# Delta-rule keys transposed with the values, key norms from squares with accumulators

## The chip, the cores and the metric

The kernel runs on one NeuronCore of a Trainium2 chip. The metric is the device time of one execution in microseconds (us). The engines are named as in the profile: PE is the matrix engine (its weight loads are listed apart as PEld), DVE the vector engine, ACT the scalar engine, POOL the GpSimd engine, SP the engine whose queue issues the transfers from memory. SBUF is the on-chip memory that they all read, PSUM the banks that PE writes.

## The reference, cut to what matters

The reference is a decoder trunk of two layers over 256 tokens of 1024 channels. Each layer has a mixer (a delta-rule branch of 8 heads and a sliding-window attention branch of 16 query heads, merged by gates) and a gated feed-forward part. The change touches the delta-rule branch only:

```python
dn_qkv = jax.nn.silu(causal_dwconv(dn_qkv, dn_conv[l]))
dq, dk, dv = [t.reshape(B, T, DN_HEADS, DN_HEAD_DIM) for t in jnp.split(dn_qkv, 3, axis=-1)]
dq, dk = l2_norm(dq), l2_norm(dk)      # x * rsqrt(sum(x*x) + EPS) over the 128 channels of a head
...
# in the chunked delta rule, S is a 128x128 state of a head:
k_dec = kc * jnp.exp(g_last[..., None] - gc)[..., None]
v_new = u_i - jnp.einsum('bhcd,bhde->bhce', w_i, S)
S = S * jnp.exp(gl)[..., None, None] + jnp.einsum('bhcd,bhce->bhde', kd, v_new)
```

The keys are needed in two layouts: channels on the partitions (as the projection leaves them, for the products of keys with keys and queries), and tokens on the partitions (for the update of the state). The norm of a key is one number per token.

## The kernel before, in words

**Projections.** Everything that is projected is computed as tiles of 128 output channels by 256 tokens. A projection tile is 24 matmuls (lines L282, L283, L284, eight times each): activations and weights are split into a high and a low part, and three products are summed into one PSUM tile `acc`. A tile's weights come by one transfer of 512 KB on the queue of SP (L200, `raw`); ACT rounds them to the high part (L210, `wH`), and DVE subtracts to get the low part (L212, `wL`). These casts run up to three tiles ahead of the products. I number the projection tiles from 0 in the order of the program, and write "tile 12, product 0" for the place just before the first matmul of tile 12. The delta rule of the first layer works beside tiles 0 to about 50; the second layer's tiles begin at 142, and its delta rule ends near tile 190.

**The work between the projections.** A convolution tile (`conv_tile`) follows each of the 24 projection tiles of queries, keys and values: two ACT copies out of PSUM (L669, L670), three DVE steps (L672), one ACT silu (L674). Values end in `vv`, queries and keys in `kq`. When the three tiles of a head exist, a job `post` is started for it; when all four heads of a half are posted, a job runs `system`, `inverse` and `solve` for the half. In between, DVE reduces the conditioning weights of the next sub-layers (L328, `raw<-raw,cact`, 128x1024, on weights from the queue of SP too), and ACT and DVE prepare the attention (`attention_prep`, L962 to L967, then L975).

**What sets the order.** Jobs are generators. After each triple of projection matmuls the program calls `tick`, which resumes the job that is due; a job yields a cost and a wait, in assumed microseconds, that decide after how many triples it is resumed. So the yields at the end of `post` and of `system` place all that follows. Priorities (`HPC`, `HPV`, `HPN`, and the engines `AB`, `VB` that raise them) decide where an instruction stands among the instructions of its own engine. Each engine then runs its list strictly in that order. Helpers that raise a priority record their instructions under one line, L278.

**post, before (L688 to L708).** For a head: ACT squares the transposed-layout keys into `k2` (128x256, shown as `k<-kq`); PE transposes the two halves of the values into a PSUM tile (L703, `ps_vt`), and multiplies the squares with a column of ones, so that the sum over channels arrives on the partitions (L705, shown as `ps_n`; two products in full precision, which the trace records as four); ACT copies the values out (`vt`), and DVE adds EPS to the two sums (`n<-ps_n`, 128x2).

**system, before (L710 to L745).** For a half: DVE makes the inverse roots and the scales from `n2`; PE multiplies keys with keys and queries for each head (L728, `ps_kk`), DVE scales these (`lq`); ACT scales the values (`vt<-vt,nk`, eight of 128x128); PE transposes the first 128 tokens of the keys of four heads (L742, `ps_kt`), and ACT scales them out of PSUM into `kw`. `kw` is read in `solve` (L863).

**PSUM.** Three pools matter: `acc` with three buffers for the projections, `ps` with three for the delta rule's products, and `pat` with two, for `ps_vt` and `ps_n2` of `post`, for the transposed queries and keys of the attention (L962, L966) and for the attention's scores (`ps_cur`, L975). A buffer is free again when its last reader is done.

## Time and profile before

| What | Value |
|---|---|
| Time of three runs, median | 1029.28 us |
| Lowest and highest | 1028.52 and 1032.02 us |
| The profiled execution, span from first to last instruction | 1029.4 us |
| Its mean granted TensorE clock | 0.995 |
| PE busy | 999.7 us |
| DVE busy | 843.6 us |
| ACT busy | 631.2 us |

The profiled execution took as long as the median run, to 0.1 us, so its span is used for the time of the kernel throughout, with nothing around it.

In a timeline, a row gives the start of an instruction, its duration, the engine, the line, the operation, the tiles that it writes and reads, and shapes; equal neighbours are joined and counted (x4). In brackets stands how long the engine was idle before, and what ended that. Durations overlap the next instruction's, so a price is the distance from one start to the next: of two projection matmuls that is 0.11 to 0.12 us, though each lasts 0.28 us.

### The profile page before, as it was taken

To read this page: it belongs to the slowest core of one execution; us is meant where nothing else is said; L and a number is where in the kernel's file an instruction comes from. 1 tells how busy PE (TensorE), PEld (TensorE's weight loads), DVE (VectorE), ACT (ScalarE), POOL (GpSimd) and SP (SyncE) were. 2 spreads that over 40 slices of the span, in tenths; PEclk is the share of its full clock that TensorE was granted. 3 is DMA by queue.
4 is the path that set the end of the run, shared out by engine and by line. 5 is a ranking of instruction groups with operands and counts; after the bars stand their busy time and mean duration, and the time that the engine had idled before them with its cause. 6 is when DMAs were issued, how large, how long until landed. Compare 5 with 4: busy or idle time off the path is not lost.

```text
span 1029.4 us, 23195 instructions
## 1 busy us (share of the span) xinstructions
PE 999.7 (97%) x9208; PEld 946.0 (92%) x9208; DVE 843.6 (82%) x1873; ACT 631.2 (61%) x1281; POOL 4.0 (0%) x8
## 2 busy tenths in 40 slices
PE   4999999999999999999999999999999999999998
PEld 2599998998899999999999999899879999999998
DVE  6799997799788898998996999986857889777653
ACT  5598675766555665564465977577554558555532
POOL 0000000000000000000000000000000000000000
PEclk9999998999999999999999999999999999999999
DMA  9875486537555478888976556762313655566661
GB/s 361 324 247 175 173 268 204 183 124 266 170 183 191 155 226 282 291 282 298 358 262 210 168 168 193 239 242 83 110 57 107 202 185 179 191 191 194 185 211 40
DMA packets 60444, 210.47 MB, mean 204 GB/s; under 512 B 6960, under 2 KB 8496, under 8 KB 60336
## 3 DMA queue, kind: packets, MB, share of 16 engines
q1 hardware_dynamic: 59904, 208.89, 61.3%
q8 instruction: 72, 1.18, 0.5%
q14 instruction: 36, 0.29, 0.1%
q10 hardware_dynamic: 432, 0.10, 0.0%
HBM read 207.92 MB, written 1.05 MB: 203 GB/s over the span
## 4 chain that ended last, share of the span: by engine, by line
PE 77%; DVE 13%; ACT 5%; DMA 2%; issue 2%; SPq 0%; DVEq 0%; ACTq 0%
PE acc L282 20%; PE acc L283 19%; PE acc L284 19%; DVE wL L212 4%; PE pa L567 4%; DMA raw<-wada 2%; ACT wH L210 2%; DVE raw L328 2%; PE ps_o L1031 1%; PE ps_kk L728 1%; DVE kq L672 1%; PE ps_cur L975 1%; PE pa L585 1%; PE pa L583 1%; PE pa L584 1%
## 5 line engine op out<-in xcount | busy, mean ns | idle before, releaser
L210 ACT CAST wH<-raw 128x1024 fp32r<-128x1024 f32 (+2 forms) x292 | 301.0, 1035 | 207.8 <-PE acc L283 130.0
L212 DVE TENSOR_TENSOR wL<-raw,wH 128x1024 fp32r<-128x1024 f32 (+2 forms) x292 | 349.3, 1200 | 76.2 <-ACT wH L210 73.3
L282 PE MATMUL acc<-hH,wH 128*128 128x256 f32 x1376 | 394.3, 287 | 0.0
L283 PE MATMUL acc<-hL,wH 128*128 128x256 f32 x1376 | 385.8, 280 | 0.0
L284 PE MATMUL acc<-hH,wL 128*128 128x256 f32 x1376 | 385.1, 280 | 0.3 <-DVE wL L212 0.2
L282 PEld LDWEIGHTS acc<-hH,wH 128*128 128x128 f32 x1376 | 259.9, 189 | 7.4 <-issue 4.3
L284 PEld LDWEIGHTS acc<-hH,wL 128*128 128x128 f32 x1376 | 260.1, 189 | 1.1 <-DVE wL L212 0.7
L283 PEld LDWEIGHTS acc<-hL,wH 128*128 128x128 f32 x1376 | 260.1, 189 | 0.7 <-issue 0.2
L328 DVE SCALAR_TENSOR_TENSOR raw<-raw,cact 128x1024 f32<-128x1024 f32 x80 | 97.1, 1219 | 9.2 <-DMA raw<-wada 9.1
L284 PE MATMUL acc<-g_b,wL 128*128 128x256 f32 x224 | 61.8, 276 | 0.0
L282 PE MATMUL acc<-g_b,wH 128*128 128x256 f32 x224 | 61.8, 276 | 0.0
L283 PE MATMUL acc<-g_b,wH 128*128 128x256 f32 x224 | 61.8, 276 | 0.0
L672 DVE SCALAR_TENSOR_TENSOR kq<-cr,pt,kq 128x255 f32<-128x255 f32 (+2 forms) x96 | 45.4, 479 | 1.5 <-ACT kq L670 1.5
L282 PEld LDWEIGHTS acc<-g_b,wH 128*128 128x128 f32 x224 | 42.1, 188 | 0.0
L283 PEld LDWEIGHTS acc<-g_b,wH 128*128 128x128 f32 x224 | 42.1, 188 | 0.0
L284 PEld LDWEIGHTS acc<-g_b,wL 128*128 128x128 f32 x224 | 42.1, 188 | 0.0
L567 PE MATMUL pa<-raw,h 128*128 128x432 f32 x96 | 37.5, 555 | 2.6 <-ACT h L473 2.6
L1192 DVE SCALAR_TENSOR_TENSOR g<-acc,pt,g 128x255 f32<-128x255 f32 x80 | 38.2, 478 | 0.6
L567 PEld LDWEIGHTS pa<-raw,h 128*128 128x128 f32 x96 | 19.2, 202 | 20.6 <-issue 17.2
L282 PE MATMUL acc<-sH,wH 128*128 128x256 f32 x128 | 36.7, 289 | 0.0
L284 PE MATMUL acc<-sH,wL 128*128 128x256 f32 x128 | 36.6, 287 | 0.0
L283 PE MATMUL acc<-sL,wH 128*128 128x256 f32 x128 | 36.5, 285 | 0.0
(329 smaller groups left out, 1964.0 us busy)
## 6 DMA issues: line engine op xcount, KB each, us to landing
raw<-wbig SPq DMA_DIRECT2D x232, 512.0 KB, 4.0
raw<-wada SPq DMA_DIRECT2D x80, 512.0 KB, 4.5
raw<-wdn SPq DMA_DIRECT2D x32, 512.0 KB, 4.5
raw<-wsa SPq DMA_DIRECT2D x24, 432.0 KB, 4.8
early<-wada SPq DMA_DIRECT2D x16, 512.0 KB, 8.5
raw<-wdn SPq DMA_DIRECT2D x16, 384.0 KB, 4.1
x<-xT SPq DMA_DIRECT2D x4, 256.0 KB, 4.2
out<-x SPq DMA_DIRECT2D x8, 128.0 KB, 3.0
```

The costliest lines, as they stand in the source:

```text
L210: A.copy(h, raw)
L212: V.tensor_tensor(lo, raw, h.bitcast(F32), ALU.subtract)
L282: PE.matmul(o, wh, ah, start=first, stop=False)
L283: PE.matmul(o, wh, al, start=False, stop=False)
L284: PE.matmul(o, wl, ah, start=False, stop=last)
L328: return V.scalar_tensor_tensor(raw, raw, 1.0, cact, op0=ALU.mult, op1=ALU.mult, accum_out=modp[l][:, f:f + 1])
L567: PE.matmul(pa[g][tb], h32[:, tb * P:tb * P + P], w, start=n == 0, stop=n == KT - 1)
L583: PE.matmul(o, hh[:, kt, sl], wh[:, k4], start=kt == 0, stop=False)
L584: PE.matmul(o, hh[:, kt, sl], wl[:, k4], start=False, stop=False)
L585: PE.matmul(o, hl[:, kt, sl], wh[:, k4], start=False, stop=kt == KT - 1)
L672: V.scalar_tensor_tensor(dst[:, sft:], cr[:, :T - sft], w_[:, 3 - sft:4 - sft], dst[:, sft:], op0=ALU.mult, op1=ALU.add)
L1192: V.scalar_tensor_tensor(g[:, sft:], pa_[:, :T - sft], fw[:, i, 2 - sft:3 - sft], g[:, sft:], op0=ALU.mult, op1=ALU.add)
```

## The change

For each of the 16 heads (8 in each of two layers) `post` now transposes the keys together with the values into one PSUM tile of four 128x128 blocks. ACT copies the values out as before, copies the first block of the keys into `kw`, and then squares each block of the keys in place in PSUM with an accumulator, which gives the sum over channels on the partitions. The square `k2` and the products with ones are gone. `n2` gets its EPS in one operation for a half, at the head of `system`. There the four transposes into `ps_kt` are gone, and `kw` is scaled in place in SBUF. `kw` has two buffers in place of one, and `pc`, a tile of the norms, three in place of four. The yields at the ends of `post` and `system` are changed with the work.

```diff
-                c = sm.tile([P, 1], F32, name="pc", bufs=4)
+                c = sm.tile([P, 1], F32, name="pc", bufs=3)
...
                     self.n2 = sm.tile([P, 2, 4], F32, name="n2", bufs=2)
-                k2 = wk.tile([P, T], F32, name="k2", tag="k2", bufs=1)
-                AB.activation(k2, kq[hd][:, 0], AF.Square)
+                    self.kw = big.tile([P, 4, P], F32, name="kw", tag="kw", bufs=2)
                 yield 0.0, POST[l]
-                pv = pat([2, P], name="ps_vt")
-                pn = pat([2], name="ps_n2")
+                pv = pat([4, P], name="ps_vt")
                 for ch in range(2):
                     PE.transpose(pv[:, ch], v_[:, ch * P:ch * P + P], C("ident"))
                 for ch in range(2):
-                    PE.matmul(pn[:, ch:ch + 1], k2[:, ch * P:ch * P + P], C("one"), start=True, stop=True)
-                AB.copy(self.vt[:, j], pv)
-                VB.tensor_scalar(self.n2[:, :, j], pn, EPS, None, op0=ALU.add)
-                yield 0.25, 0.5
+                    PE.transpose(pv[:, 2 + ch], kq[hd][:, 0, ch * P:ch * P + P], C("ident"))
+                AB.copy(self.vt[:, j], pv[:, 0:2])
+                AB.copy(self.kw[:, j], pv[:, 2])
+                for ch in range(2):
+                    AB.activation(pv[:, 2 + ch], pv[:, 2 + ch], AF.Square, accum_out=self.n2[:, ch, j:j + 1])
+                yield 0.44, 0.5
...
                 n2 = self.n2
+                VB.tensor_scalar(n2, n2, EPS, None, op0=ALU.add)
...
-                kw = self.kw = big.tile([P, 4, P], F32, name="kw", tag="kw")
-                pv = ps([4, P], name="ps_kt")
+                kw = self.kw
                 for j in range(4):
-                    PE.transpose(pv[:, j], kq[hf * 4 + j][:, 0, 0:P], C("ident"))
-                for j in range(4):
-                    AB.activation(kw[:, j], pv[:, j], AF.Identity, scale=kws[:, j:j + 1])
-                yield 0.45, 0.0
+                    AB.activation(kw[:, j], kw[:, j], AF.Identity, scale=kws[:, j:j + 1])
+                yield 0.0, 0.0
```

Since the yields and the instructions are others, the scheduler's lists differ in more places than these. Three of them are shown. A row is an instruction of one engine's list: line, operation, tiles, shape, and how many follow each other. Line numbers of the changed kernel are one higher or two lower than before there: L701 and L703 are the transposes of values and keys, L729 the key products, L960 the transposed queries (L962 before), L973 the scores (L975 before), L785 and L792 the products in the inverse (L787 and L794 before).

The first place is PE's list in layer 0, from the second to the third post and on to the transposed queries of the attention. Before, from tile 10, product 16:

```order
L703 MATMUL ps_vt<-ct,vv 128x128 x2
...
L705 MATMUL ps_n_841<-ct,k_762 128x1 x2
...
L703 MATMUL ps_vt<-ct,vv 128x128 x2
...
L705 MATMUL ps_n_966<-ct,k_887 128x1 x2
...
L962 MATMUL ps_qT<-ct,tok 128x128 x8
```

In the changed kernel, from tile 11, product 3:

```order
L701 MATMUL ps_vt<-ct,vv 128x128 x2
L703 MATMUL ps_vt<-ct,kq 128x128 x2
...
L960 MATMUL ps_qT<-ct,tok 128x128 x8
```

Before, 66 projection matmuls stand between the last norm products and the transposed queries, which come at tile 14, product 10; in the changed kernel the queries come 21 projection matmuls after the third post, at tile 12, product 0, and the second block of them moved from tile 18, product 14, to tile 16, product 8.

The second place is PE's list in layer 0 ahead of the attention's first scores, where the last products of the first half's 32-blocks stand. Before:

```order
L794 MATMUL ps_z_2089<-u_1527,yt_2064 32x32 x32
L283 MATMUL acc<-hL,wH 128x256
L284 MATMUL acc<-hH,wL 128x256
L282 MATMUL acc<-hH,wH 128x256
L283 MATMUL acc<-hL,wH 128x256
L284 MATMUL acc<-hH,wL 128x256
L975 MATMUL ps_cur_2181<-kT,qT 128x128
```

In the changed kernel, with 24 projection matmuls between the first and the last row, of which the first two are shown:

```order
L792 MATMUL ps_z_2079<-u_1516,yt_2054 32x32 x32
L282 MATMUL acc<-hH,wH 128x256
L283 MATMUL acc<-hL,wH 128x256
...
L973 MATMUL ps_cur_2169<-kT,qT 128x128
```

The scores stand at tile 32, product 3, in both; the four groups of 32 products ahead of them moved from tiles 30 and 31 (at 30.3, 30.8, 31.18 and 31.22) to tiles 28 to 31 (28.6, 28.21, 30.12 and 31.3).

The third place is DVE's list in layer 1, around the convolution of the values that the second post of the second half transposes. Before:

```order
L212 TENSOR_TENSOR wL<-raw,wH 128x1024
L672 SCALAR_TENSOR_TENSOR vv<-cr,pt,vv 128x255
L278 STREAM_TRANSPOSE ut_8926<-u_8601 128x256
L672 SCALAR_TENSOR_TENSOR vv<-cr,pt,vv 128x254
L328 SCALAR_TENSOR_TENSOR raw,modp_105<-raw,cact 128x1024
L672 SCALAR_TENSOR_TENSOR vv<-cr,pt,vv 128x253
```

In the changed kernel:

```order
L328 SCALAR_TENSOR_TENSOR raw,modp_105<-raw,cact 128x1024
L278 TENSOR_TENSOR uc<-uc,nb 128x8x2
L672 SCALAR_TENSOR_TENSOR vv<-cr,pt,vv 128x255
L278 TENSOR_TENSOR nb<-nb,uc 128x8
L212 TENSOR_TENSOR wL<-raw,wH 128x1024
L672 SCALAR_TENSOR_TENSOR vv<-cr,pt,vv 128x254
L278 TENSOR_TENSOR uc<-uc,nb 128x8
L328 SCALAR_TENSOR_TENSOR raw,modp_105<-raw,cact 128x1024
L672 SCALAR_TENSOR_TENSOR vv<-cr,pt,vv 128x253
```

The three steps of the values begin one weight cast earlier and have two conditioning reductions among and ahead of them in place of one; the block transpose `ut` and most of `u` moved behind them. PE's transposes of these values moved from tile 166, product 21, to tile 167, product 0.

## The prediction

> **What bounds the kernel now.** I read the page's busy times and its chain first.
>
> ```profile
> span 1029.4 us, 23195 instructions
> PE 999.7 (97%) x9208; PEld 946.0 (92%) x9208; DVE 843.6 (82%) x1873; ACT 631.2 (61%) x1281; POOL 4.0 (0%) x8
> ...
> q8 instruction: 72, 1.18, 0.5%
> ...
> PE 77%; DVE 13%; ACT 5%; DMA 2%; issue 2%; SPq 0%; DVEq 0%; ACTq 0%
> PE acc L282 20%; PE acc L283 19%; PE acc L284 19%; DVE wL L212 4%; PE pa L567 4%; DMA raw<-wada 2%; ACT wH L210 2%; DVE raw L328 2%; PE ps_o L1031 1%; PE ps_kk L728 1%; DVE kq L672 1%; PE ps_cur L975 1%; PE pa L585 1%; PE pa L583 1%; PE pa L584 1%
> ```
>
> PE is busy for 97%, and 58% of the chain are projection matmuls. So PE time taken out is worth its full size wherever PE is not waiting, and nothing where it waits for DVE or ACT. Which of the two holds in the stretches that the change touches is a question for the stages (columns: stretch, length, then busy time and count of PE, PEld, DVE, ACT, POOL; granted clock, DMA share, GB/s).
>
> ```profile
> 57.00:80.00 23.00, 22.75 (x196) 22.35 (x196) 22.32 (x54) 22.19 (x55) 0.00 (x0) 1.00 0.67 230
> 132.00:165.00 33.00, 32.43 (x500) 30.84 (x499) 32.45 (x85) 20.88 (x41) 0.00 (x0) 1.00 0.83 275
> 620.00:650.00 30.00, 29.31 (x239) 28.67 (x238) 28.07 (x82) 21.55 (x48) 0.00 (x0) 1.00 0.65 200
> ...
> 167.10:173.90 6.80, 6.39 (x86) 5.61 (x84) 5.54 (x14) 1.27 (x4) 0.00 (x0) 0.50 0.38 133
> 651.80:655.20 3.40, 3.40 (x18) 3.40 (x17) 2.55 (x5) 2.01 (x4) 0.00 (x0) 0.50 0.84 222
> ```
>
> While the first heads are prepared (57 to 80 us), ACT is busy for 22.19 of 23 us and DVE for 22.32; from 132 to 165 us DVE is busy for 32.45 of 33. In these stretches three engines are full together, so a second saved on PE can turn into a wait. The last two rows are stretches in which the granted clock was 0.50: matmuls then cost twice as much, so these 6.80 and 3.40 us did the work of about half: 3.4 and 1.7 us are lost there. The waits of PE in the two layers' delta rule (57 to 180 us, then 560 to 700 us):
>
> ```profile
> PE ps_cur L975 <- issue: 1.6, 1, 1.6
> PE ps_qT L962 <- DVE tok L954: 1.5, 1, 1.5
> ...
> PE acc L284 <- DVE wL L212: 0.2, 1, 0.2
> ...
> PE ps_vt L703 <- ACT vv L674: 2.9, 2, 2.3
> ```
>
> And the two waits that stand ahead of the slow stretches, in the timeline, with what DVE does there:
>
> ```profile
> 164.38 0.71 PE L975 MATMUL ps_cur<-kT,qT 64*128 64x128 f32 x6
> 166.71 1.13 PE L975 MATMUL ps_cur<-kT,qT 64*128 64x128 f32 x10 [1.62 <-issue]
> ...
> 169.19 1.06 PE L820 MATMUL ps_y<-ut,lq 32*32 32x32 f32 x32 [0.41 <-DVE ut L278]
> ...
> 167.46 1.23 DVE L328 SCALAR_TENSOR_TENSOR raw<-raw,cact 128x1024 f32<-128x1024 f32 x1 [2.81 <-DMA raw<-wada]
> ...
> 651.58 0.55 PE L703 MATMUL ps_vt<-ct,vv 128*128 128x128 f32 x2 [2.27 <-ACT vv L674]
> ...
> 649.40 1.22 DVE L328 SCALAR_TENSOR_TENSOR raw<-raw,cact 128x1024 f32<-128x1024 f32 x1
> ```
>
> The first wait is for nothing that the profile shows. I read it as instructions that came late: 9208 matmuls and as many loads in 72 packets of the instruction queue are 256 instructions each, and they are used up faster ahead of this place (500 matmuls in the 33 us from 132 us, 15 per us) than in most (196 in 23 us, 9 per us). The second is the values of a head, late because a conditioning reduction (649.40) stands among their steps on DVE. About each such wait there is a clock of 0.50 for 3.4 or 6.8 us, so a wait of 2 us costs 4 to 5.
>
> [...]
>
> **The change part by part.** *PE.* Prices are distances between starts, around a post and around the old key transposes:
>
> ```profile
> 665.34 0.38 PE L703 MATMUL ps_vt<-ct,vv 128*128 128x128 f32 x2
> 665.56 0.51 PE L705 MATMUL ps_n<-ct,k 128*128 128x1 f32 x4
> 665.92 0.36 PE L282 MATMUL acc<-hH,wH 128*128 128x256 f32 x1
> ...
> 123.06 0.60 PE L742 MATMUL ps_kt<-ct,kq 128*128 128x128 f32 x4
> 123.42 0.36 PE L282 MATMUL acc<-hH,wH 128*128 128x256 f32 x1
> ```
>
> A post costs 665.92 − 665.34 = 0.58 us. Four transposes cost 123.42 − 123.06 = 0.36 us, per half, so 0.09 per head. Together 0.67 per head before. After, a post is four transposes, 0.36, and the old group is gone: 0.31 saved per head, 5.0 us over 16 heads. Bounds: where the two parts of a post stood apart, the products alone took 0.36 (665.92 − 665.56), and the key transposes added take half of 0.36: 0.36 + 0.09 − 0.18 = 0.27, or 4.3 us; at the most 5.4, as the matmul after a post or group is itself a little late.
>
> *ACT and DVE*, for the same head:
>
> ```profile
> 85.49 0.42 ACT L278 ACTIVATE k<-kq 128x256 f32<-128x256 f32 x1
> 85.80 0.38 ACT L278 COPY vt<-ps_vt 128x256 f32<-128x256 f32 x1
> ...
> 52.48 0.27 ACT L591 COPY vtok<-pa 128x128 f32<-128x128 f32 x1
> 52.64 0.19 ACT L587 COPY ab<-pa 128x16 f32<-128x16 f32 x1
> ...
> 178.32 0.49 ACT L278 ACTIVATE s<-s,nm,rq 128x128 f32<-128x128 f32 x1
> 178.71 0.19 ACT L278 ACTIVATION_READ_ACCUMULATOR s<-s,nm,rq 128x1 f32 x1
> 178.80 0.49 ACT L278 ACTIVATE s<-s,nm,rq 128x128 f32<-128x128 f32 x1
> ...
> 118.92 0.16 DVE L278 TENSOR_SCALAR n<-ps_n 128x2 f32<-128x2 f32 x1 [1.38 <-PE ps_n L705]
> 119.11 0.17 DVE L278 TENSOR_SCALAR nk<-n 128x8 int32<-128x8 int32 x1
> ```
>
> The square of 128x256 that goes was 85.80 − 85.49 = 0.31 us. The copy into `kw` is priced by a copy of 128x128 out of PSUM, 0.16. A square of 128x128 with an accumulator has no row. The nearest is the exponential of 128x128 with an accumulator, 0.48 from start to start; it reads its scale and bias from memory, and the square does not. From below stands the copy, 0.16, and the read of the accumulator, 178.80 − 178.71 = 0.09: 0.25. I take 0.40, nearer to the upper, same-shaped row. Net per head 0.16 + 2 × 0.40 − 0.31 = +0.65 us, between +0.35 and +0.81, over 16 heads +10.4 us. [...] On the whole ACT has room for it (61% busy), but three heads of each layer fall into stretches like the one from 57 us, with 0.8 us free.
>
> DVE loses 12 of 16 small additions, 0.1 to 0.2 us each by the rows, 1 to 2 us in all, and the wait for `ps_n` (1.38 us here) goes from the path of the weight casts behind it. `kw` is scaled in the same count of ACT instructions as before; I count nothing. The buffers of `pc` and `kw` cost nothing: ACT keeps its order with `pc` in any case, and two `kw` only loosen.
>
> *What takes some of it back.* (a) The transposed queries moved up to tile 12, right behind the third post. They need both buffers of the PSUM pool that `post` uses, and the second square of that post now stands behind a weight cast on ACT; where PE had a `tok` wait of 1.5 us at the second block before, I expect about 1.0 at the first and 1.0 at the second: +0.5 us, from 0 (the waits only change place) to +1.6. (b) ACT's long run of scalings for the first half now stands ahead of the cast of tile 22, in place of 23. This is the tightest place for weights, already in the trace:
>
> ```profile
> 131.80 1.23 DVE L212 TENSOR_TENSOR wL<-raw,wH 128x1024 fp32r<-128x1024 f32 x1 [0.17 <-ACT wH L210]
> 132.71 0.28 PE L283 MATMUL acc<-hL,wH 128*128 128x256 f32 x1
> 133.08 0.39 PE L284 MATMUL acc<-hH,wL 128*128 128x256 f32 x1
> ```
>
> PE's L284 comes at 133.08, straight after `wL` ends at 133.03 and 0.25 late. By then the change has saved PE 0.22 on each of five posts and one old group, 5 × 0.22 + 0.36 = 1.5 us, and here it can lose them again; DVE gets back the 1.38 us wait. I take +0.7, from −0.3 (the present two delays vanish) to +1.6. (c) The 2.27 us wait in layer 1 is set by DVE, which is full there (28.07 of 30 us). In layer 1 too PE has saved five posts and one old group by then, 1.5 us, so it arrives early and waits. I take most of that, +1.0, from 0 to +1.9. (d) Half of b's scalings in front of tile 36: +0.2, from 0 to +1.
>
> *The first wait.* The groups of 32 products that use up instructions fastest stand some 25 projection matmuls further apart and earlier in the new list, and the counts ahead of the scores changed, so that the border between two instruction packets no longer need fall on the scores. If the wait of 1.6 us goes, PE reaches the next product (169.19) earlier, and there `ut` may be late, as DVE waited 2.81 us for a transfer ahead of it; but that product's input `u` is computed 19 projection matmuls earlier too. Bounds: nothing gained (the border falls on another group, or `ut` takes the wait over), or 1.6 + 3.4 = 5.0 us gained. I take half, −2.5.
>
> Sum: −5.0 + 0.5 + 0.7 + 1.0 + 0.2 − 2.5 = −5.1, which from 1029.4 gives 1024.3 us. The profiled execution is 0.1 us from the runs' median of 1029.28, so this is forecast for the median too.
>
> **The rivals.** *No change that can be told (1026.2 to 1032.4).* A measurement of this kernel can tell 0.3%, 3.1 us. The wait for instructions stays or finds another place, and the terms (a) to (d) come out as above: 1029.4 − 5.0 + 2.4 = 1026.8; with a little more of them, 1028. For it: DVE's 32.45 of 33 us and ACT's 22.19 of 23 us. Against it: most of the 16 posts lie where PE waits for nothing.
>
> *Slower: ACT keeps PSUM occupied.* The place is tile 12 of layer 0. If a square costs the full 0.48, ACT has 3 × 0.81 = 2.4 us more to do for the three posts, in a stretch that had 0.8 us free; the transposed queries then wait up to 2.4 us for the pool's buffers. That is as long as the waits which brought a clock of 0.50 at 167 and 652 us, and brings two such windows more, 3.4 us. With the wait for instructions in place: 1029.4 − 5.0 + 2.4 − 0.5 + 2.4 + 3.4 = 1032.1; with one more window in layer 1, where the second half's value wait can lengthen in the same manner, 1.7 more, 1033.8. It decides from a wait of about 1.6 us on, the shortest that the trace shows with a slow stretch behind it. Against it: PE also arrives with its own `tok` wait there, which covers part.
>
> *A larger gain.* The wait for instructions goes with its slow stretch, and the wait in layer 1 falls short enough to leave the clock at full: −5.0 + 1.4 − 5.0 − 1.7 = −10.3, 1019.1 us. For it: both are single events that hang on an exact place in the order. Against it: DVE has as much work ahead of the values in layer 1 as before, and now two reductions.
>
> **How the numbers follow.** Forecast (1021 to 1026.2) 0.42; larger gain 0.12; no change 0.27; slower 0.19, of which a part lies only just beyond 1032.4. So faster by over 0.3% has 0.54, within 0.27, slower 0.19. The time is the forecast's, 1024.3, with its own range of 1021 to 1026.2. The whole range takes in the larger gain's end and most of the slower case: 1018.8 to 1033.
>
> **What would show it.** Right: 96 fewer PE and PEld instructions together, a post as one group of four transposes at 0.36 us; ACT about 10 us busier and DVE 1 to 2 us less; no wait for `issue` before the scores, and a clock of 1.00 from 165 to 180 us. Wrong: a wait at the transposed queries of tile 12 for ACT's squares of more than 1.6 us; a low clock near 92 us; waits of L284 for `wL` near 130 us of over 1.6 us; a wait for `vv` in layer 1 above 3 us; or a wait for `issue` elsewhere. The forecast falls if PE's busy time drops by the 5 us and its idle time rises by as much.

## The result, and the profile after

The changed kernel is slower. Over six runs of each, taken together, it has a median of 1037.8 us (1037.0 to 1040.76) against 1032.05 us (1028.52 to 1033.32): a ratio of 1.0071, with a 95% interval from 1.0047 to 1.0094. The forecast was 1024.3 us, and 0.19 had been given to any slower outcome. One thing about the scale was wrong besides: a run's time is not its span, but 1.7 to 2.1 us more (the profiled execution after has a span of 1036.9 us and a time of 1038.83). So the forecast of 1024.3 us, which starts from a span, is about 1026.2 us as a time, and the kernel before takes 1032.05 us as a median of six, not 1029.28. Neither changes which way the forecast missed. Below, spans are compared with spans and times with times.

From the page of the changed kernel, its span, busy times, chain and the group of the conditioning reductions (busy time and mean of one in ns, then the idle time of DVE ahead of them, and what ended it):

```profile
span 1036.9 us, 23126 instructions
PE 996.4 (96%) x9160; PEld 942.5 (91%) x9160; DVE 841.1 (81%) x1861; ACT 637.1 (61%) x1345; POOL 4.0 (0%) x8
...
PE 72%; DVE 12%; ACT 6%; DMA 6%; issue 3%; SPq 0%; DVEq 0%; ACTq 0%
...
L328 DVE SCALAR_TENSOR_TENSOR raw<-raw,cact 128x1024 f32<-128x1024 f32 x80 | 97.4, 1219 | 21.4 <-DMA raw<-wada 21.3
```

The same group on the page of before, which the prediction did not show:

```profile
L328 DVE SCALAR_TENSOR_TENSOR raw<-raw,cact 128x1024 f32<-128x1024 f32 x80 | 97.1, 1219 | 9.2 <-DMA raw<-wada 9.1
```

PE has 48 matmuls and 48 loads fewer and DVE and ACT have changed by little, but the chain now goes through transfers for 6% instead of 2%. The reductions do the same work on the same 80 tiles, and DVE stands in front of them for 21.3 us instead of 9.1.

**Where the time is.** I cut each span into what PE worked at full clock, what it lost at a lower clock (length times one less the clock, stretch by stretch; in the profile of before, projection matmuls start 0.21 us apart at a clock of 0.50, and 0.11 to 0.12 at 1.00), and what it was idle: before 994.6 + 5.1 + 29.7, after 989.6 + 6.8 + 40.5. So the change took 5.0 us of work out of PE, as forecast, and 10.8 us of idle time and 1.7 of slow clock came in. By projection tiles most of the loss is in three places: tiles 24 to 37 (+1.6), 124 to 130 (+4.1) and 172 to 178 (+3.6). The second has nothing to do with the delta rule; between tiles 57 and 149 the lists of all engines are those of before. The profile of before had a slow stretch of its own in tiles 24 to 37 (a clock of 0.50 for 6.8 us). Against the second profile of before (run before2 below), which has none, the two profiles of the changed kernel take 4.4 and 2.1 us more there, and 2.5 and 3.2 us more at tiles 172 to 178.

The waits of PE in layer 0 (57 to 250 us) of the changed kernel:

```profile
PE ps_y L818 <- DVE ut L278: 2.4, 1, 2.4
...
PE acc L284 <- DVE wL L212: 1.5, 1, 1.5
...
PE ps_qT L960 <- DVE tok L952: 0.5, 1, 0.5
```

The wait for `issue` ahead of the scores is gone, but the next product now waits 2.4 us for `ut`. The timeline of that place:

```profile
164.68 1.22 DVE L328 SCALAR_TENSOR_TENSOR raw<-raw,cact 128x1024 f32<-128x1024 f32 x1 [1.51 <-DMA raw<-wada]
...
166.25 1.23 DVE L212 TENSOR_TENSOR wL<-raw,wH 128x1024 fp32r<-128x1024 f32 x1
167.40 0.34 DVE L278 SCALAR_TENSOR_TENSOR u<-ps_z,ct,u 128x128 f32<-128x128 f32 x1
167.66 1.22 DVE L328 SCALAR_TENSOR_TENSOR raw<-raw,cact 128x1024 f32<-128x1024 f32 x1
168.80 0.44 DVE L278 STREAM_TRANSPOSE ut<-u 128x256 f32<-128x256 f32 x1
...
169.39 0.77 PE L818 MATMUL ps_y<-ut,lq 32*32 32x32 f32 x32 [2.44 <-DVE ut L278]
```

DVE stands 1.51 us at a reduction whose weights have not landed. What is behind it in DVE's list, `u` and `ut` among it, is late by that, and PE waits. (A second reduction stands between `u` and `ut`; its weights are there, and it adds its own 1.2 us.) The waits view puts this down to `ut`; only the row ahead shows the transfer. At tile 124 it is the same with a weight cast behind the reduction:

```profile
487.26 1.23 DVE L328 SCALAR_TENSOR_TENSOR raw<-raw,cact 128x1024 f32<-128x1024 f32 x1 [2.37 <-DMA raw<-wada]
...
489.14 1.22 DVE L212 TENSOR_TENSOR wL<-raw,wH 128x1024 fp32r<-128x1024 f32 x1
...
490.42 0.38 PE L284 MATMUL acc<-g_a,wL 128*128 128x256 f32 x1 [2.87 <-DVE wL L212]
```

**The place in layer 1 that every profile of the changed kernel shows.** DVE around the values of the last heads, before:

```profile
675.34 1.23 DVE L212 TENSOR_TENSOR wL<-raw,wH 128x1024 fp32r<-128x1024 f32 x1
676.48 0.48 DVE L672 SCALAR_TENSOR_TENSOR vv<-cr,pt,vv 128x255 f32<-128x255 f32 x1
...
677.89 0.44 DVE L672 SCALAR_TENSOR_TENSOR vv<-cr,pt,vv 128x253 f32<-128x253 f32 x1
678.25 1.22 DVE L328 SCALAR_TENSOR_TENSOR raw<-raw,cact 128x1024 f32<-128x1024 f32 x1
...
680.54 1.28 DVE L278 SCALAR_TENSOR_TENSOR s<-ct,ps_cur 128x512 f32<-128x512 f32 x2
```

and in a second profile of the changed kernel (the run "again" below), with the PE row that follows:

```profile
675.02 0.45 DVE L278 STREAM_TRANSPOSE ut<-u 128x256 f32<-128x256 f32 x1
677.98 1.23 DVE L328 SCALAR_TENSOR_TENSOR raw<-raw,cact 128x1024 f32<-128x1024 f32 x1 [2.51 <-DMA raw<-wada]
...
679.13 0.48 DVE L672 SCALAR_TENSOR_TENSOR vv<-cr,pt,vv 128x255 f32<-128x255 f32 x1
...
682.20 0.47 DVE L672 SCALAR_TENSOR_TENSOR vv<-cr,pt,vv 128x253 f32<-128x253 f32 x1
682.59 1.28 DVE L278 SCALAR_TENSOR_TENSOR s<-ct,ps_cur 128x512 f32<-128x512 f32 x2
...
683.42 0.41 PE L701 MATMUL ps_vt<-ct,vv 128*128 128x128 f32 x2 [3.07 <-DVE s L278]
```

Before, the three steps of the values came first and the reduction behind them, with its weights there. Now a reduction stands ahead of the values and waits 2.51 us. The values and the scores `s` behind it are late, and the scores are what empties the two PSUM buffers of the pool that `ps_vt` needs: PE stands 3.07 us. A row of the windows view, from the start of tile 172 to the start of tile 178, gives the price; tile 178 itself takes 9.0 us in both (columns: length; PE busy; PEld, DVE, ACT, POOL; clock, DMA share, GB/s). Before:

```profile
670.31:702.56 32.25, 31.85 (x444) 28.66 (x442) 24.46 (x65) 25.91 (x63) 0.00 (x0) 1.00 0.55 187
```

and again:

```profile
669.25:705.85 36.60, 32.43 (x385) 29.23 (x377) 23.87 (x62) 26.85 (x70) 0.00 (x0) 0.95 0.46 153
```

36.60 against 32.25 us: 3.8 us more idle and 5% of the clock.

**What moved.** The transfers are issued in the same order, and land in a median of 4.6 us (4.5 before). But the scheduler put nine reductions of the first layer, the fourth to the twelfth, one to three weight casts earlier in DVE's list, and some others later. Seven of the nine, the fifth to the eleventh of this queue, start at tiles 21, 21, 26, 28, 30, 30, 31 before, and at tiles 20, 21, 24, 25, 28, 28, 30 now. From the issue of the transfer to the reduction these seven had 11.8, 12.1, 7.3, 11.4, 6.3, 7.4 and 5.3 us before; now they have 3.5, 4.3, 4.5, 5.1, 4.9, 4.1 and 5.2. Against a landing time of 4.6 us that is no margin. In layer 1 six of the last 16 moved one or two casts earlier. DVE's waits for these transfers rose from 5.0 to 8.3 us in the first 32 reductions, from 3.1 to 4.6 in the next 32, whose place did not change, and from 0.9 to 8.4 in the last 16.

### The profile page after: what moved, and what is told of

It is laid out like the page before. It is cut to its first block, busy times and chain, and to the rows that moved or that the text cites. A ratio compares the mean times of both kernels' runs of the same rounds, so it can differ in the third digit from the quotient of the medians.

```text
span 1036.9 us, 23126 instructions
## 1 busy us (share of the span) xinstructions
PE 996.4 (96%) x9160; PEld 942.5 (91%) x9160; DVE 841.1 (81%) x1861; ACT 637.1 (61%) x1345; POOL 4.0 (0%) x8
## 4 chain that ended last, share of the span: by engine, by line
PE 72%; DVE 12%; ACT 6%; DMA 6%; issue 3%; SPq 0%; DVEq 0%; ACTq 0%
PE acc L282 19%; PE acc L283 19%; PE acc L284 19%; DMA raw<-wada 5%; DVE wL L212 5%; PE pa L567 3%; ACT wH L210 2%; DVE raw L328 2%; DVE kq L672 1%; PE ps_kk L729 1%; PE ps_o L1029 1%; PE ps_cur L973 1%; PE pa L585 1%; PE pa L584 1%; PE pa L583 1%
## 5 line engine op out<-in xcount | busy, mean ns | idle before, releaser
L284 PE MATMUL acc<-hH,wL 128*128 128x256 f32 x1376 | 385.7, 280 | 1.5 <-DVE wL L212 1.5
L284 PEld LDWEIGHTS acc<-hH,wL 128*128 128x128 f32 x1376 | 260.3, 189 | 1.9 <-DVE wL L212 1.7
L328 DVE SCALAR_TENSOR_TENSOR raw<-raw,cact 128x1024 f32<-128x1024 f32 x80 | 97.4, 1219 | 21.4 <-DMA raw<-wada 21.3
L284 PE MATMUL acc<-g_b,wL 128*128 128x256 f32 x224 | 61.8, 276 | 0.0
L284 PEld LDWEIGHTS acc<-g_b,wL 128*128 128x128 f32 x224 | 42.0, 188 | 0.0
L284 PE MATMUL acc<-g_a,wL 128*128 128x256 f32 x128 | 36.2, 283 | 2.9 <-DVE wL L212 2.9
L284 PE MATMUL acc<-sH,wL 128*128 128x256 f32 x128 | 36.6, 287 | 0.0
```

Source lines behind the costliest of these rows:

```text
L284: PE.matmul(o, wl, ah, start=False, stop=last)
L328: return V.scalar_tensor_tensor(raw, raw, 1.0, cact, op0=ALU.mult, op1=ALU.mult, accum_out=modp[l][:, f:f + 1])
```

## The experiments

Four theories are named in the expectations. **A**: PE's products of the delta rule were put in worse places, by the changed yields. **B**: ACT's squares with accumulators hold PSUM and delay what follows. **C**: when a transfer lands differs from one execution to the next, and the first profile was unlucky. **D**: reductions stand in DVE's list ahead of steps that PE needs, and these steps are late while DVE stands at the reductions' transfers (2.51 us in the rows of "again" above). A ratio is to the kernel before, timed beside the run. "Waits" is the sum of DVE's waits for `raw<-wada` in the one execution that was profiled, 9.1 us before and 21.3 after; waits and tiles are of that execution, times and ratios of all.

### The same kernel again, and the kernel before again

No edit.

> The changed kernel once more, for a second trace. In the first one 4.05 us of the loss stand at tiles 124 to 130 of layer 0 (a wait of L284 for wL at 487 us and a clock of 0.50 behind it), where the order of every engine is the same as before. Theory C (the wait is set by when transfers land, which differs from one execution to the next): it is absent or at another tile, and the span falls by about 4 us in that execution. Rival (it follows from the exact times at which the earlier stretch ends): it is there again, 3.0 to 3.3 us at the same tile. Time against the kernel before: ratio 1.004 to 1.009 by both.

Measured: 1038.98 us, ratio 1.0075 (1.0046 to 1.0103); waits 21.0. In the profile, of 1032.5 us, PE's wait at tile 124 is absent, though DVE still stands 1.6 us at the reduction there (2.4 in the first profile), and tiles 124 to 130 take 0.2 us less than before; tiles 172 to 178 take 4.4 more. So C holds for tile 124, 4 us of the first profile; the place in layer 1 comes back. The profiled execution was the fastest of its four (1034.4 us, the others 1037.62 to 1040.71), so how often tile 124 costs its 4 us is not shown.

> The kernel before once more, for a second trace. Theory D (the saved PE time is lost where DVE, strictly in order, stands at a conditioning reduction whose weights have not landed, with steps behind it that PE needs): as in the first trace, no wait of a reduction for its transfer at tiles 172 to 175 of layer 1, and the stretch from tile 172 to 178 takes 32 to 33 us. If it takes 35 to 37 us as in the four other kernels, the first trace of before was only a lucky one there. Ratio 1.

Measured: 1027.63 us in one execution, clock 1.00 throughout, waits 9.3; tiles 172 to 178 take 1.2 us more than in the first profile of before (33.4 us to the start of tile 178, a little over the forecast, with a reduction that waits 0.7 us). The waits' sums, 9.1 and 9.3 before, 21.3 and 21.0 after, go with the kernel more than with the execution.

### The yields of before in the changed kernel, and the reverse

The first is the yield at the end of `post`, the second that of `system`.

```diff
-                yield 0.44, 0.5
+                yield 0.25, 0.5
...
-                yield 0.0, 0.0
+                yield 0.45, 0.0
```

> The changed kernel with the yields of before (0.25 behind post, 0.45 at the end of system), nothing else. It puts PE's list of layer 1 back to the places of before, and leaves layer 0's first half as in the changed kernel. Theory A (the loss comes from where PE's products are placed, ahead of what they wait for): layer 1, tiles 150 to 188, gets back 3 to 5 us, and the ratio falls to 0.999 to 1.003. Theory B (ACT is late, by 10 us of squares with accumulators and copies): layer 1 stays within 1 us of the changed kernel, ratio 1.005 to 1.009.

Measured: 1039.48 us, 1.0074 (1.0046 to 1.0101); waits 20.9. Most of PE's products in layer 1, among them those of keys with keys, are then back in their places of before; the posts and the transposed queries are not, and the reductions stand where the changed kernel has them, to one weight cast. Tiles 172 to 178 still take 4.9 us more. A's forecast missed, as far as this edit tests it.

The reverse is the kernel before with the yields 0.44 and 0.0, and nothing else changed.

> The kernel before with the changed kernel's yields (0.44 behind post, 0.0 at the end of system), and no other change. Same work on every engine as before. Theory A: the other places alone cost 1 to 5 us, ratio 1.001 to 1.005. Theory B: no ACT work is added, so within 1 us of before, ratio 0.999 to 1.001.

Measured: 1037.27 us, 1.0059 (1.0037 to 1.0081); waits 13.6. In its timeline the same picture stands, without a square or a transposed key:

```profile
676.97 1.23 DVE L328 SCALAR_TENSOR_TENSOR raw<-raw,cact 128x1024 f32<-128x1024 f32 x1 [1.53 <-DMA raw<-wada]
...
678.12 0.48 DVE L672 SCALAR_TENSOR_TENSOR vv<-cr,pt,vv 128x255 f32<-128x255 f32 x1
...
682.61 0.66 PE L703 MATMUL ps_vt<-ct,vv 128*128 128x128 f32 x2 [1.88 <-DVE s L278]
```

Two numbers that move the lists cost the kernel before nearly as much as the whole change costs (1.0059 and 1.0071), and at this place by the same order on DVE. So a loss of this size needs none of the operations that the change adds. A's forecast of a loss came true here, though above its range; the yields alone do not explain the changed kernel, which lost as much with the yields of before.

### Only the norms

The changed kernel, with the transposes into `ps_kt` and the scaling out of PSUM of before for `kw`, and with the yield of before at the end of `system`:

```diff
-                AB.copy(self.kw[:, j], pv[:, 2])
...
+                kw = self.kw = big.tile([P, 4, P], F32, name="kw", tag="kw")
+                pv = ps([4, P], name="ps_kt")
...
+                    PE.transpose(pv[:, j], kq[hf * 4 + j][:, 0, 0:P], C("ident"))
...
+                yield 0.45, 0.0
```

> The changed kernel without the second part of the change: keys are transposed with the values and squared with accumulators for the norms, but kw is made as before by four transposes of its own per half and scaled out of PSUM, and the copy into kw is gone. PE 0.36 us per half more than the changed kernel (1.4 us in all), ACT 2.5 us less. Theory A: the ratio depends on the places; the first queries stand at tile 14.0 and 17.2 in place of 12.0 and 16.3, so layer 0, tiles 12 to 37, loses less; ratio 1.000 to 1.005. Theory B: the squares are still there, ratio 1.005 to 1.010.

Measured: 1036.1 us, 1.0051 (1.0032 to 1.0069; one execution of the seven took 1436.78 us and is not in the ratio); waits 14.1. In layer 1 PE waits 4.5 us for `vv` and 2.7 for `s` ahead of the transposes of `post`. The loss comes with this part already; it does not tell B from D.

### No transfers for the reductions

In both kernels the 80 transfers are left out, and the reductions read a vector that lies in SBUF; the conditioning is thus not computed, and all instructions of DVE, ACT and PE stay.

```diff
+    def ada_dot2(l, f, raw):
+        return V.scalar_tensor_tensor(raw, cact, 0.001, cact, op0=ALU.mult, op1=ALU.mult, accum_out=modp[l][:, f:f + 1])
...
-            nc.sync.dma_start(raw, wada[l, f])
...
-                dot = ada_dot(l, g * 8 + f, raw)
+                dot = ada_dot2(l, g * 8 + f, raw)
```

> The kernel before without the 80 transfers of conditioning weights after the start: the reductions (L328) run in the same number and size on data that lie in SBUF already, so what is left out is the transfers and the true conditioning values. Theory D: DVE's waits for these transfers (9.2 us in all in the first trace of before) go, and the kernel is 0 to 6 us faster than before, ratio 0.994 to 1.000.

> The changed kernel with the same left out as in nodma_before. Theory D: the waits for conditioning weights (21.4 us in the first trace of the changed kernel) go, so what PE saves is left: 3 to 6 us faster than nodma_before. Theory A (the places of PE's products cost the time whatever DVE waits for) or theory B (ACT's squares): still 3 to 8 us slower than nodma_before.

Measured: before 1030.56 us (1029.42 to 1031.03), ratio 0.9988 (0.997 to 1.0007); after 1025.52 us (1024.85 to 1026.11), 0.9951 (0.9935 to 0.9968). The runs do not overlap: with nothing to wait for, the change is worth 5.0 us by the medians and 3.8 us by the ratios. The forecast's saving on PE was 5.0, but the match is in part luck: in the two profiles PE works 8.6 us less and is idle 2.2 us more. The pages, without transfers, before:

```profile
span 1029.1 us, 23035 instructions
PE 998.3 (97%) x9208; PEld 943.0 (92%) x9208; DVE 842.2 (82%) x1873; ACT 632.4 (61%) x1281; POOL 4.0 (0%) x8
```

and after:

```profile
span 1023.1 us, 22966 instructions
PE 990.1 (97%) x9160; PEld 936.1 (91%) x9160; DVE 841.3 (82%) x1861; ACT 638.8 (62%) x1345; POOL 4.0 (0%) x8
```

Up to the start of tile 178, tiles 172 to 178 take 32.01 us after, without transfers (32.25 in before). DVE's rows of that place, with the PE row that follows (lines one to three higher than in the changed kernel):

```profile
670.89 1.22 DVE L331 SCALAR_TENSOR_TENSOR raw<-cact 128x1024 f32<-128x1024 f32 x1
...
672.07 0.48 DVE L673 SCALAR_TENSOR_TENSOR vv<-cr,pt,vv 128x255 f32<-128x255 f32 x1
...
673.19 1.22 DVE L331 SCALAR_TENSOR_TENSOR raw<-cact 128x1024 f32<-128x1024 f32 x1
...
677.83 0.41 PE L702 MATMUL ps_vt<-ct,vv 128*128 128x128 f32 x2 [1.09 <-DVE s L278]
```

Here too two reductions stand ahead of and among the steps of the values, and cost DVE their 1.2 us each. Without a wait for a transfer PE is idle for 1.1 us from tile 172 to the end of tile 178, where it is idle for 3.4 and 4.2 us in the two profiles of the changed kernel (0.4 and 1.4 before). So it is mostly the wait that costs there, and not the reductions' work. In this run without transfers ACT does all its squares and holds PSUM as it does in the slow kernel. PE's posts stand within one tile of their places in the changed kernel. So A and B fell, and what is left is the transfers: D, or the memory traffic itself. In both kernels tiles 52 to 124 take 5.5 to 5.8 us more without these transfers (PE waits for weight casts at tiles 85 to 109), since the lists differ there too; so a gain against before is not read from this pair, only the difference of the two.

### Another due time for the reductions in layer 1

```diff
-ADC = ((2, 3, 2, 2), (3, 1, 3, 2))
+ADC = ((2, 3, 2, 2), (3, 1, 0, 2))
```

> The changed kernel with three conditioning reductions of layer 1 moved: the number behind the third head of the second half goes from 3 to 0, and they are made up later, where nothing of the delta rule is near. Theory D: the two reductions that stand among the values and scores at tiles 172 to 175, with 4.0 and 3.5 us of waits for transfers in the two traces, are gone from there, and the stretch from tile 172 to 178 falls from 36 to 32 or 33 us: ratio 1.002 to 1.005. Theory B: no change, ratio 1.006 to 1.009.

Measured: 1038.48 us, 1.0076 (1.0061 to 1.0091); waits 18.8. Tiles 172 to 178 take 6.3 us more than before; PE waits 4.4 us for `s`. A miss: the reductions that were taken from one group of tiles gathered in another.

### A third transfer in flight

```diff
-            while adaq and len(adaf) < 2:
+            while adaq and len(adaf) < 3:
```

> The changed kernel with the transfers of conditioning weights issued one step earlier: three are in flight ahead of their reductions in place of two, with the same six buffers. Theory D (what PE saves is lost because the reductions on DVE now stand closer behind the issue of their transfers): the waits of reductions for transfers fall from 21 us to under 10, and the ratio to 0.995 to 1.002. If instead the buffers are short, weights come late and the waits of wL and wH for transfers grow by as much: ratio 1.003 to 1.010.

> The kernel before with the same edit, as the control. It has only 9 us of such waits, so theory D expects little: ratio 0.997 to 1.002. It is slower if the six buffers are short.

Measured: 1045.61 us after, 1.0173 (1.0128 to 1.0218), and 1045.31 before, 1.016 (1.0128 to 1.0192). DVE's waits fell in the changed kernel, to 12.9 us, and the two kernels came level, but both lose 12 to 13 us at tiles 52 to 124. PE waits there for weight casts (`acc` L284 for `wL`, 4.4 us in all after). The reductions' tiles and the projections' weights share their buffers, which is the likely cause, but it is not shown: from 250 to 480 us ACT waits 31.3 us for the transfers of weights, and 31.6 in the changed kernel.

A miss as a remedy; it shows only that a transfer issued earlier costs these kernels more than it gives the reductions.

### The reductions held behind a weight cast

Each reduction gets an order on DVE behind the low part that was made four before the newest. The data stay the same. What is set is the place in DVE's list; the issue of the transfers follows it, as buffers come free later (the fifth is issued at 125.9 us, and at 118.7 in the changed kernel).

```diff
-        V.tensor_tensor(lo, raw, h.bitcast(F32), ALU.subtract)
+        lows.append(V.tensor_tensor(lo, raw, h.bitcast(F32), ALU.subtract))
...
                 dot = ada_dot(l, g * 8 + f, raw)
+                after(dot, lows[-4])
```

> The changed kernel with each conditioning reduction held, in DVE's order, behind the low part of the weights that was made four tiles' worth before the newest; the issue of the transfers is not moved by hand. In DVE's list the reductions of layer 0 and 1 then stand 0 to 5 weight casts later than in the changed kernel. Theory D: their waits for transfers fall from 21 us to under 10, and the ratio to 0.995 to 1.002. Rival (the reductions hold the buffers longer, so that weights are late): ratio 1.003 to 1.010.

> The kernel before with the same edit, as the control: theory D expects little, ratio 0.997 to 1.003.

Measured: after 1030.86 us, 1.0007 (0.998 to 1.0034), waits 6.8; before 1030.94, 1.0005 (0.9978 to 1.0033), waits 6.1. The order alone takes the loss against before away (1.0007 where the changed kernel had 1.0071 and 1.0075), and does nothing for the kernel before, whose reductions stood well. This is D's own test: work and transfers are the same, and the order on DVE is not. But the change's 5 us do not come out. Tiles 172 to 178 still take 3.2 us more than before, and PE waits there 2.96 us for `s`; reductions still wait 0.6 and 1.1 us ahead of it. In the kernel before, held alike, these tiles take 4.3 us more, with a reduction that waits 1.4 us and a mean clock of 0.91, so this place does not by itself keep the two level.

### Held in one layer only

The first 32 of the reductions fed through this queue work for layer 0, the last 16 for the second part of layer 1. For layer 0 alone `lows[-4]` is used for the first 32 and `lows[-8]` for the others; for layer 1 alone `lows[-8]` is used for the first 64 and `lows[-2]` for the last 16. For layer 0 alone:

```diff
+                nd['n'] += 1
+                after(dot, lows[-(4 if nd['n'] <= 32 else 8)])
```

and for layer 1 alone

```diff
+                nd['n'] += 1
+                after(dot, lows[-(8 if nd['n'] <= 64 else 2)])
```

> The changed kernel with the conditioning reductions held on DVE in layer 0 alone (the first 32 of them, as in hold4). Theory D says that what holding them gave back (7 us, from 1.0075 to 1.0007) is shared by the layers as the waits are: layer 0 has 10 of the changed kernel's 21 us of waits for transfers. Ratio 1.002 to 1.005.

> The changed kernel with the reductions held in layer 1 alone (the last 16, two weight casts more than in hold4). They have 8 us of the waits, the 3.5 us at the start of layer 1's attention and the waits at tiles 172 to 175 among them. Theory D: ratio 1.001 to 1.005, and the wait of L701 for the scores on DVE at tile 174 (3.0 us in hold4) under 1.5 us, as no reduction stands ahead of the scores any more.

Measured: layer 0 alone 1033.78 us, 1.0009 (0.9985 to 1.0033), waits 9.7, tiles 172 to 178 +6.4 us; layer 1 alone 1028.83 us, 0.9964 (0.9936 to 0.9992), waits 8.2, tiles 172 to 178 −0.7. The sums of the waits differ by 1.5 us, the times by 5.0, so the sum alone does not give the time. Both are below the changed kernel and below what was expected. But the layers are not cleanly parted, for `lows[-8]` binds too: with layer 1 alone four reductions of layer 0 stand up to five casts later, and the waits of the first 32 fall from 8.3 to 3.9 us; with layer 0 alone the longest wait of layer 1 falls from 3.5 to 0.5 us. How the loss is shared between the layers is therefore not shown.

### Held in both, each by its own distance

In both kernels, `lows[-4]` for the first 32 and `lows[-2]` for the last 16:

```diff
+                after(dot, lows[-(4 if nd['n'] <= 32 else 8 if nd['n'] <= 64 else 2)])
```

> The changed kernel with both: layer 0 as in hold4, layer 1 two casts more. Theory D: the sum of both gains, and with the wait at tile 174 gone some of the 5 us of PE work that the change takes out shows: ratio 0.995 to 1.000. If something else than the reductions holds PE there: as hold4, 0.999 to 1.003.

> The kernel before with the same edit as mix42, the control: 0.998 to 1.002 by theory D, as it loses little to these waits. The difference to mix42 is what the change is worth with the reductions out of the way: 2 to 5 us in favour of the changed kernel.

Measured: after 1028.48 us (1025.72 to 1030.78), 0.997 (0.9944 to 0.9996), waits 4.6; before 1031.1 us (1028.28 to 1033.89), 0.9978 (0.9957 to 0.9999), waits 4.9. The place of layer 1 in the held, changed kernel (line numbers are four higher for PE's products and the convolution, one higher for the helper):

```profile
673.14 0.45 DVE L279 STREAM_TRANSPOSE ut<-u 128x256 f32<-128x256 f32 x1
673.51 1.18 DVE L212 TENSOR_TENSOR wL<-raw,wH 128x1024 fp32r<-128x1024 f32 x1
674.61 0.47 DVE L676 SCALAR_TENSOR_TENSOR vv<-cr,pt,vv 128x255 f32<-128x255 f32 x1
675.01 1.22 DVE L329 SCALAR_TENSOR_TENSOR raw<-raw,cact 128x1024 f32<-128x1024 f32 x1
...
678.08 1.27 DVE L279 SCALAR_TENSOR_TENSOR s<-ct,ps_cur 128x512 f32<-128x512 f32 x2
...
678.90 0.41 PE L705 MATMUL ps_vt<-ct,vv 128*128 128x128 f32 x2 [0.46 <-DVE s L279]
```

No reduction waits, and PE's wait is 0.46 us instead of 3.07. From the start of tile 172 to the start of tile 178 it takes 31.53 us:

```profile
668.12:699.65 31.53, 31.06 (x384) 27.96 (x377) 23.32 (x62) 26.25 (x70) 0.00 (x0) 1.00 0.52 171
```

This version beats the changed kernel by 9 us and the kernel before by 0.3% (0.04% to 0.56%), of which the kernel before, held alike, shows 0.22% too. It is no faster than layer 1 alone (1028.83 us, 0.9964), so the sum of both gains that was expected did not come. Between the two held kernels the change is worth 2.6 us by the medians, ± 1.5 by the spread of the ten runs of each, but only 0.8 us by the ratios; its size is not settled. In the two profiles PE works 7.8 us less after and is idle 4.6 us more (34.0 us against 29.4).

## Why the prediction was wrong, point by point

**PE's saving was right in its step.** A post is one group of four transposes, and 96 instructions went. The row after it starts 108.49 − 108.13 = 0.36 us behind its first, as forecast:

```profile
108.13 0.38 PE L701 MATMUL ps_vt<-ct,vv 128*128 128x128 f32 x2
108.35 0.38 PE L703 MATMUL ps_vt<-ct,kq 128*128 128x128 f32 x2
108.49 0.37 PE L282 MATMUL acc<-hH,wH 128*128 128x256 f32 x1
```

Between the first two profiles the work at full clock fell by 5.0 us. Its total is less certain than that: the pairs before2 and again, the two of mix42 and the two without transfers give 6.8, 7.8 and 8.6 us.

**ACT's price was too high, and it did not matter.** The estimate was 0.40 us for a square with accumulator. ACT's timeline has it:

```profile
85.86 0.27 ACT L278 COPY kw<-ps_vt 128x128 f32<-128x128 f32 x1
86.01 0.29 ACT L278 ACTIVATE ps_vt<-ps_vt 128x128 f32<-128x128 f32 x1
86.20 0.20 ACT L278 ACTIVATION_READ_ACCUMULATOR ps_vt<-ps_vt 128x1 f32 x1
86.29 0.38 ACT L278 COPY vt<-ps_vt 128x256 f32<-128x256 f32 x1
```

From the square's start to the next work it takes 0.28 us, and ACT became 5.9 us busier, where +10.4 was forecast. So the rival "ACT keeps PSUM occupied" had the right sign and about half of the loss (1032.1 to 1033.8, 2.7 to 4.4 us over its start, where the ratio of 1.0071 is 7.3), by a mechanism that is not there: at tile 12 the transposed queries wait 0.5 us, less than the 1.5 of before.

**The small terms.** (a) was +0.5 and came out as a wait 1.0 us shorter at that place. (b), the `wL` wait at tile 22, is 1.5 us against 0.2, +1.3 where +0.7 was taken and 1.6 was the bound; in the second profile it is 0.9. (c), the wait for `vv` in layer 1, taken as 1.0 us longer than 2.27, is 1.8 in one execution and 3.28 in the other. In the first no reduction among the values waits; in the second DVE stands 1.09 us at one. So the price fits one execution, and what makes the difference is a transfer. (d), +0.2 at tile 36, is not seen. All four together are small beside what was missed.

**The first wait.** The wait for `issue` ahead of the scores went, as forecast (before, it is 1.62 us, and 0.89 in the second profile). That it was a wait for instructions was an estimate from the page's counts; no run shows it. But the lower bound was what happened: `ut` took the wait over, with 2.44 us and a clock of 0.50 for 3.4 us behind it. In the second profile it takes over 0.7 us only. The prediction had named this, and had weighed against it that `u` is computed earlier on the new list. It had quoted DVE's wait of 2.81 us for a transfer at this very place, and had not asked whether the new list has such a wait as well.

**The step that failed.** It is a term missing from "what takes some of it back": DVE's waits for the transfers of the reductions that the new lists put earlier stand there at nothing. The third place of the lists showed two conditioning reductions ahead of and among the steps of the values, where one had stood. The prediction took (c) from a DVE that is full, named the two reductions only against the larger gain, and counted no wait with them. A reduction costs there its 1.2 us and whatever is still missing of its transfer's 4.6 us, and what stands behind it on DVE pays. No term of the sum and no rival held this, though the page of before had 9.1 us of it in its group of reductions. The runs showed 21.3 us of it after; with these transfers left out of both kernels the changed one is 5.0 us the faster, and with the reductions held to later places it gives back 9 us. The condition "the forecast falls if PE's busy time drops by the 5 us and its idle time rises by as much" was met, with 10.8 us.

What stays open: which of the scheduler's costs put the reductions earlier; how the loss is shared between the layers; why tiles 124 to 130 take 3.1 to 3.3 us more in the profiles of both last kernels than in the first of before (five of the 18 profiles take 3 to 4 us more there, most take none); and how much of the 5.0 us the held kernel shows.

## What to carry to other kernels

When a change moves the lists, look in the new lists for every instruction that is fed by a transfer and stands ahead of steps that another engine needs, and compare the time since its transfer's issue (5 to 12 us for the seven above, before) with the landing time (4.6 us); its own duration, 1.2 us here, can be the smaller part of its price beside a wait of 1.5 to 2.5 us. A wait that a view puts down to a step of the engine next door may be a transfer two rows ahead in that engine's list. And an experiment that moves the lists and changes no work (here two yields) shows what a reordering alone costs, before the new operations are blamed.

## What the runs showed of the hardware

Without the 80 transfers of 512 KB, ten runs of the kernel before lie within 1.6 us (1029.42 to 1031.03) at a granted clock of 0.999 or 1.000; with them, 13 runs of the same kernel beside these range from 1028.11 to 1036.01. I had not expected that most of the spread between executions goes with these transfers.

The clock fell after single waits of PE of 1.62 us (before, at 167 us, with a clock of 0.50 behind it) to 3.07 us, and also after two short waits together. In the second profile of the changed kernel, windows around the wait of 3.07 us at 680 us:

```profile
680.00:683.40 3.40, 0.35 (x3) 0.16 (x3) 3.40 (x7) 0.61 (x2) 0.00 (x0) 1.00 0.78 217
683.40:686.80 3.40, 3.38 (x46) 3.10 (x47) 3.40 (x16) 3.19 (x10) 0.00 (x0) 0.66 0.70 255
686.80:690.20 3.40, 3.40 (x29) 3.18 (x28) 3.37 (x12) 2.47 (x9) 0.00 (x0) 0.84 0.49 151
```

This wait costs its 3.07 us and, by the clocks of the two windows behind it, 3.4 × (0.34 + 0.16) = 1.7 us more. In the first profile of the changed kernel, waits of 1.12 and 0.80 us stand in one window:

```profile
146.00:149.40 3.40, 1.62 (x13) 1.21 (x11) 3.36 (x14) 3.40 (x8) 0.00 (x0) 1.00 0.72 253
149.40:152.80 3.40, 3.26 (x74) 3.19 (x75) 2.68 (x5) 1.23 (x7) 0.00 (x0) 0.50 0.61 171
```

Here 1.78 idle us of 3.40 stood ahead of a clock of 0.50. The length of one wait does not decide it: the wait of 2.01 us at 678 us of this profile was followed by a clock of 0.50; the one of 1.80 us at 656 us was not (1.00 from 650 to 660 us), nor was the one of 2.1 us in the second profile of before (1.00 throughout). What decides it, no run shows.
